# Branch B's K and Q turned by VectorE blocks and a trip through DRAM instead of by TensorE, in a two-layer mixer block

## The chip, the cores and the metric

The kernel runs on one core of one Trainium2 chip, as a single launch. The metric is the time of that launch on the device in microseconds (us). TensorE is PE in the rows, VectorE DVE, ScalarE ACT, GpSimd POOL and SyncE SP; PEld is the load of the stationary operand of a matmul.

## The reference, cut to what matters

Two layers act on 512 tokens of width 1024: 256 context tokens and 256 tokens of x. Each layer norms its input, multiplies it by one wide matrix w_in, and feeds three branches: A is a gated linear recurrence (mLSTM), B a differential attention, C a two-dimensional Fourier mix. The branches are merged through sigmoid gates and multiplied by w_out. The last layer returns x alone, so there only the x tokens have queries. Branch B, which the change touches:

```python
qh = apply_axial_rope(rmsnorm(q.reshape(b, n, 8, 2, 64), q_norm_w))   # 8 heads, 2 maps of 64 features
kh = apply_axial_rope(rmsnorm(k.reshape(b, n, 8, 2, 64), k_norm_w))
s = einsum('bhmqd,bhmkd->bhmqk', q, k) * 64 ** -0.5
p = softmax(s)
w = p[:, :, 0] - lam * p[:, :, 1]
o = einsum('bhqk,bhkv->bhqv', w, v)
y_b = rmsnorm(o, subln_w) * (1 - lam_init) * silu(bz)
...
y = g_a * (y_a @ w_a_out) + g_b * (y_b @ w_b_out) + g_c * (y_c @ w_c_out)
```

## The kernel before, in words

**Numbers.** Every fp32 operand of a large product is split into a high and a low float32r part, and a product is three matmuls (high by high, low by high, high by low). A split is a cast on ScalarE and a subtraction on VectorE (`split`).

**Main stream.** The weights come in pieces of 512 rows by 256 columns: a DMA of SP into `raw`, the cast `wh` on ScalarE, the subtraction `wl` on VectorE. A piece is multiplied with the 512 tokens (the last 256 in parts of layer 1) into one of three PSUM banks, whose tiles are called `pm`. The main stream goes through the branches in the order of ORDER0 and ORDER1; in layer 1 that is "A0 B0 A1 B1 A2 A3 C0 B2 B3 M0 C1 C2 C3 M1 M2 W0". A digit is a group of 256 columns; M0, M1 and M2 are the three merges (of branches A, B and C), W0 the last product.

**Side work.** What is no main product (branch B's scores and softmax, branch A's recurrence, branch C's transforms) is written as Python generators, which are launched when their projections are done. They use five other PSUM banks, whose tiles are called `ps`. While the program is written out, `Clocks` books each instruction on its engine at an estimated cost; after each main step `tick` lets a generator take its next step when the time it asked for (`when`) has been reached by the estimated TensorE clock. The order so found is fixed: every engine executes its own queue in that order, and waits on semaphores where the estimate was off. Every other engine's instruction is recorded by one helper (L161), every matmul at L232, every transpose on TensorE at L236.

**Branch B's side generator** is `b_side(g)`, for a group g of two heads. K and Q lie token-major, in [128 tokens, tiles, 256 features]. After norm and rope, `qk_transpose` turns them for one head: four transposes on TensorE (two for Q in layer 1) into a PSUM bank, and a split from the bank into `kT` and `qT`. For each query tile follow six matmuls of scores in two banks, the softmax (maximum on VectorE, exponential on ScalarE, the weighted difference `Pt` on VectorE), the transposes of `Pt` into `W` on TensorE, and the product `pv` of eight matmuls with V. A product pv comes up to LAG = 3 items behind its scores. At the end GpSimd makes the scale `os` of the outputs (tile `Q` in layer 1, where O lies in Q's place), VectorE applies it, TensorE transposes the outputs, and VectorE multiplies them into `Gb`, which is branch B's part of the merge.

**The merge** of branch i first runs its gates (products of `hTh`, `hTl` with weights) where AHEAD is 1, which it is for M1 of layer 1, then the products of the branch's output `y` with w_x_out. Between the two stands

```python
drain(recs)
```

which writes out all that is left of the branch's four side generators, one after the other, with no main step between.

**Memory.** `gen` hands out slots of one ring of SBUF tiles, NGEN = 28 of them, to all larger intermediates.

Of the kernel before, what the change touches and what calls it, by code (L numbers as in the profile page):

```python
# [27 lines left out]
NGEN = 28  # L28
# [4 lines left out]
ACTIVE = 5  # L33
# [8 lines left out]
ORDER1 = "A0 B0 A1 B1 A2 A3 C0 B2 B3 M0 C1 C2 C3 M1 M2 W0"  # L42
AHEAD = ((0, 1, 1), (1, 1, 0))
# [47 lines left out]
class Clocks:  # L91
    """When each engine gets to what is emitted, estimated, to place the side work among the main products."""
# [34 lines left out]
class Paced:  # L127
    """An engine whose instructions are booked as they are emitted."""
# [38 lines left out]
def hybrid_kernel(ctx: ExitStack, tc: tile.TileContext, t):  # L167
# [78 lines left out]
    # ------------------------------------------------------------- constants  # L246
# [117 lines left out]
    # ------------------------------------------------------------- adaLN  # L364
    def ada_bias(l, piece):
        """b_ada of 1024 columns in the first two rows of a tile of zeros"""
        brow = gen([128, 1024], F32, "brow")
        gpsimd.memset(brow, 0.0)
        gpsimd.dma_start(out=brow[0:2, :],
                            in_=t["b_ada"][l:l + 1, 512 * piece:512 * piece + 1024].to_broadcast([2, 1024]))  # L370
        return brow

    def ada_rows(l, piece, dma):
        """w_ada of 512 columns"""
        raws = []
        for q in range(4):
            r = gen([128, 2, 512], F32, "adaw")
            dma(out=r, in_=t["w_ada"][l, 256 * q:256 * (q + 1), 512 * piece:512 * (piece + 1)]
                .rearrange("(k p) f -> p k f", p=128))
            raws.append(r)  # L380
        return raws

    def ada_mm(raws, brow, dst):
        """sc @ w_ada + b_ada: partitions 32 g + stream hold four partial sums"""
        ps = ps_side()
        for k in range(KT):
            g = k % 4
            mm(ps[32 * g:32 * g + 32, :], sct[:, k, :], raws[k // 2][:, k % 2, :], k < 4, k >= 4)
        vector.tensor_tensor(dst, ps, brow, op=ALU.add)
# [8 lines left out]
    def ada_finish(l, pc, ks=slice(0, 8)):  # L398
        """pc: shift and scale of some blocks of features"""
# [9 lines left out]
    def ada_gen(l, pieces):  # L409
        """shift and scale columns (pieces 0..3) as a side generator"""  # L410
# [34 lines left out]
    # ------------------------------------------------------------- norm -> feature-major h  # L445
# [3 lines left out]
    def norm_stats(tiles):  # L449
        """normalized copies of some token tiles"""  # L450
# [10 lines left out]
    def norm_apply(l, i, src, base):  # L461
        """src: the normalized transposed blocks base .. base + 3 of token tile i; returns the closing step"""
# [23 lines left out]
    # ------------------------------------------------------------- weight pieces  # L486
# [74 lines left out]
    def fm_chunk(rhs, evac, ntok, bank=ps_main, step=4):  # L561
        """two 128-column blocks of W, feature-major: out[block][128 cols, tokens]"""
# [24 lines left out]
    def tm_chunk(lhs, tiles, evac, single=False, step=4):  # L587
        """256 columns of W, token-major: out[pair][128 tokens, 2, 256]"""
# [24 lines left out]
    # ------------------------------------------------------------- side machinery  # L613
# [4 lines left out]
    def launch(g):  # L618
        rec = {"g": g, "due": 0.0, "done": False}
        side.append(rec)  # L620
        return rec
# [8 lines left out]
    def tick():  # L630
        pe0 = clocks["pe"]
        for rec in list(side[:ACTIVE]):
# [12 lines left out]

    def hrhs(t0, n):
# [7 lines left out]
    # ============================================================= one layer  # L654
    def layer(l, P):
# [8 lines left out]
        def packed(name, i):  # L664
            """[128, 2, NTOK], two of them in a slot where they fit"""
# [6 lines left out]
        # ---------- branch A: gates  # L672
        def gates_side():
            """kind x head i of the gate preactivations: from column 32 x + i, token-major, to a partition"""
# [71 lines left out]
        # ---------- branch A: heads  # L746
# [72 lines left out]
        def a_side(h):  # L819
# [97 lines left out]
            for dh in range(2):  # L917
# [9 lines left out]
        # ---------- branch B  # L927
# [58 lines left out]
        def b_side(g):  # L986
# [25 lines left out]

            def qk_transpose(X, nt, n, name):
                ps = ps_side()
                for i in range(nt):
                    transpose(ps[:, 128 * i:128 * i + 128], X[:, i, 128 * hd:128 * hd + 128], ident)
                T = gen([128, 2, n], F32R, name)
# [6 lines left out]
            def softmax(hd, i, p2, n):  # L1024
                """the weighted difference of both maps, short of the first one's 1 / sum"""
# [8 lines left out]
                for m_ in range(2):  # L1034
# [9 lines left out]
                                               op0=ALU.mult, op1=ALU.add)  # L1044
                return Pt, ri, when(Pt)

            def w_transpose(Pt, n):
                ps = ps_side()
                for k in range(n // 128):
                    transpose(ps[:, 128 * k:128 * k + 128], Pt[:, 0, 128 * k:128 * k + 128], ident)  # L1050
                W = gen([128, 2, 512], F32R, "W")
# [18 lines left out]
            for it in items + [None] * LAG:  # L1070
                cur = None
                if it is not None and it[1] == 0:
                    hd = it[0]
                    kT = qk_transpose(K, 4, 512, "kT")
# [8 lines left out]
                if it is not None:  # L1083
# [13 lines left out]
                    pend.append((hd, i, Pt, at, n, ri[:, 0:1]))  # L1097
# [10 lines left out]
            for hd in range(2):  # L1108
# [8 lines left out]
        # ---------- branch C  # L1117
        def c_proj(g):
# [3 lines left out]
            def evu(a, pr, ps):  # L1122
                """sums and differences of features d and d + 128"""
# [64 lines left out]
        # ---------- merge  # L1188
        yacc = {}

        def merge(recs, ahead, key, first, final):
            ys = {}

            def split_y(q):
                ys[q] = gen_pair([128, 2, NTOK], "y")
                split(ST[key].pop(q), ys[q][0], ys[q][1])

            def spread(g, every):
                """split a y that is there after each so many steps"""
# [19 lines left out]
            drain(recs)  # L1219
# [65 lines left out]
    # ============================================================= program  # L1285
# [34 lines left out]
    # ---- start: the first products follow the adaLN columns, a quarter of the features at a time  # L1320
# [33 lines left out]
    def turn(q, hold=False):  # L1354
        """x, feature-major"""
# [13 lines left out]
    def quarter(q):  # L1369
        """the scale and shift of a quarter of the features, and what they make of x"""  # L1370
# [47 lines left out]
    def do(L, l, kind, i):  # L1418
# [10 lines left out]
        elif kind == "M":  # L1429
            recs = [ST[("a", "b", "c")[i], g]["rec"] for g in range(4)]  # L1430
            mo = [j for k, j in order[l] if k == "M"]
            run(L["merge"](recs, AHEAD[l][i], ("ya", "yb", "yc")[i], mo.index(i) == 0, mo.index(i) == 2))
# [63 lines left out]
```

## Time and profile before

| | |
|---|---|
| time, median of 3 runs | 1522.76 us (1522.59 to 1523.91) |
| span of the profiled execution | 1521.1 us, 25867 instructions |
| busy in it: TensorE | 1499.1 us, 99% |
| VectorE | 971.5 us, 64% |
| ScalarE | 735.0 us, 48% |
| GpSimd | 145.7 us, 10% |
| DMA, mean | 126 GB/s |

The span goes from the first to the last instruction of the profiled execution. No time of its own is given for that execution; the median of the runs is 1.7 us above its span. Busy times of TensorE overlap from one matmul to the next (each starts before the one ahead has ended), so the time that a matmul takes of the engine is read from the distance of starts.

### The profile page before, as it was taken

What the parts mean: (1) busy time and instruction counts of PE and PEld (TensorE: products, weight loads), DVE (VectorE), ACT (ScalarE), POOL (GpSimd) and SP (SyncE); (2) the same over time, 40 slices, a digit from 0 to 9 for tenths busy, and PEclk for the clock granted to TensorE, in tenths of its full rate; (3) what the DMA queues carried; (4) which work ended last, traced back from release to release, by engine and by line L of the source; (5) the groups of instructions that cost most, each with busy time, mean ns of one, the idle gap of its engine ahead of it and who ended that gap; (6) DMA issues with size and microseconds to landing.
All of it is one profiled execution on the core that took longest, in us unless ns stands there. A gap on an engine that the chain in (4) does not pass through costs nothing.

```text
span 1521.1 us, 25867 instructions
## 1 busy us (share of the span) xinstructions
PE 1499.1 (99%) x10410; PEld 1350.8 (89%) x10410; DVE 971.5 (64%) x1833; ACT 735.0 (48%) x1384; POOL 145.7 (10%) x193
## 2 busy tenths in 40 slices
PE   6999999999999999999999999999999999999999
PEld 4888889999998987897786789999999999999998
DVE  3447666677677586436664367677687666977765
ACT  4443556544544545334432235545557554656443
POOL 4001000020100010001024001001020011000200
PEclk9999999999999999999999999999999999999999
DMA  9524333332222222223249337544344523545754
GB/s 310 167 84 127 87 94 105 105 97 70 75 67 69 70 84 70 84 84 97 70 144 337 78 112 228 139 131 133 115 111 118 167 84 109 169 139 153 256 162 151
DMA packets 181611, 192.07 MB, mean 126 GB/s; under 512 B 9818, under 2 KB 174612, under 8 KB 181492
## 3 DMA queue, kind: packets, MB, share of 16 engines
q1 hardware_dynamic: 170080, 159.93, 35.6%
q0 software_dynamic: 7936, 27.27, 5.9%
q10 hardware_dynamic: 3476, 3.23, 0.7%
q8 instruction: 81, 1.33, 0.4%
q14 instruction: 38, 0.31, 0.1%
HBM read 188.23 MB, written 2.17 MB: 125 GB/s over the span
## 4 chain that ended last, share of the span: by engine, by line
PE 92%; DVE 3%; SPq 2%; issue 1%; ACT 1%; DMA 1%; ACTq 0%; DVEq 0%
PE pm L232 76%; PE ps L232 13%; PE ps L236 3%; SPq L161 2%; DVE wl L161 1%; DVE Rx L161 1%; DMA raw<-in_w_in_dram 0%; DVE Rc L161 0%; DMA prow<-in_a_norm_w_dram 0%; DVE lfm L161 0%; DVE at L161 0%; ACT lse L161 0%; DVE Ga L161 0%; ACT wh L161 0%; DVE ntmp L161 0%
## 5 line engine op out<-in xcount | busy, mean ns | idle before, releaser
L161 DVE TENSOR_TENSOR wl<-raw,wh 128x1024 fp32r<-128x1024 f32 x280 | 340.9, 1223 | 193.4 <-ACT wh L161 192.8
L161 ACT CAST wh<-raw 128x1024 fp32r<-128x1024 f32 x280 | 293.6, 1054 | 169.0 <-PE pm L232 135.0
L232 PE MATMUL pm<-hTh,wh 128*128 128x256 f32 (+1 forms) x1008 | 349.0, 346 | 0.0
L232 PE MATMUL pm<-hTl,wh 128*128 128x256 f32 (+1 forms) x1008 | 342.8, 340 | 0.0
L232 PE MATMUL pm<-hTh,wl 128*128 128x256 f32 (+1 forms) x1008 | 342.4, 340 | 0.0
L232 PE MATMUL pm<-wh,hTh 128*128 128x256 f32 (+1 forms) x1152 | 329.8, 286 | 1.5 <-DVE Ga L161 0.8
L232 PE MATMUL pm<-wl,hTh 128*128 128x256 f32 (+1 forms) x1152 | 324.1, 281 | 0.7 <-DVE wl L161 0.7
L232 PE MATMUL pm<-wh,hTl 128*128 128x256 f32 (+1 forms) x1152 | 324.2, 281 | 0.3 <-DVE hTl L161 0.2
L232 PEld LDWEIGHTS pm<-wh,hTh 128*128 128x128 f32 x1152 | 217.3, 189 | 10.4 <-issue 5.5
L232 PEld LDWEIGHTS pm<-wl,hTh 128*128 128x128 f32 x1152 | 216.9, 188 | 2.1 <-DVE wl L161 1.0
L232 PEld LDWEIGHTS pm<-wh,hTl 128*128 128x128 f32 x1152 | 217.5, 189 | 0.7 <-DVE hTl L161 0.7
L232 PEld LDWEIGHTS pm<-hTh,wh 128*128 128x128 f32 x1008 | 189.7, 188 | 30.8 <-issue 9.9
L232 PEld LDWEIGHTS pm<-hTh,wl 128*128 128x128 f32 x1008 | 189.5, 188 | 23.3
L232 PEld LDWEIGHTS pm<-hTl,wh 128*128 128x128 f32 x1008 | 189.7, 188 | 19.0
L232 PE MATMUL pm<-y,wh 128*128 128x512 f32 (+1 forms) x768 | 192.7, 342 | 0.0
L232 PEld LDWEIGHTS pm<-y,wh 128*128 128x128 f32 x768 | 128.9, 188 | 18.3 <-issue 2.6
L232 PE MATMUL pm<-y,wl 128*128 128x512 f32 (+1 forms) x384 | 129.4, 337 | 0.0
L161 ACT ACTIVATE Pt<-ps,mx,qsc 128x512 f32<-128x512 f32 (+1 forms) x96 | 67.1, 706 | 27.7 <-DVE mx L161 22.0
L232 PEld LDWEIGHTS pm<-y,wl 128*128 128x128 f32 x384 | 72.2, 188 | 8.6
L232 PE MATMUL pm<-wh,yf 128*128 128x256 f32 x384 | 73.0, 287 | 0.0
L232 PEld LDWEIGHTS pm<-wh,yf 128*128 128x128 f32 x384 | 59.9, 188 | 0.3
L161 DVE TENSOR_REDUCE mx<-ps 128x1 f32<-128x512 f32 (+1 forms) x96 | 53.0, 593 | 4.3 <-PE ps L232 4.2
(243 smaller groups left out, 1969.8 us busy)
## 6 DMA issues: line engine op xcount, KB each, us to landing
raw<-in_w_in_dram SPq DMA_DIRECT2D x192, 512.0 KB, 3.7
adaw<-in_w_ada_dram POOLq DMA_DIRECT2D x32, 512.0 KB, 7.1
raw<-in_w_out_dram SPq DMA_DIRECT2D x24, 512.0 KB, 4.5
adaw<-in_w_ada_dram SPq DMA_DIRECT2D x16, 512.0 KB, 8.5
raw<-in_w_in_dram SPq DMA_DIRECT2D x32, 256.0 KB, 3.3
raw<-in_w_a_out_dram SPq DMA_DIRECT2D x16, 512.0 KB, 3.4
raw<-in_w_c_out_dram SPq DMA_DIRECT2D x32, 256.0 KB, 3.4
raw<-in_w_b_out_dram SPq DMA_DIRECT2D x16, 512.0 KB, 3.8
```

What stands on the lines that cost most here:

```text
L161: return f(*a, **k)
L232: nc.tensor.matmul(out=o, lhsT=a, rhs=b, start=start, stop=stop)
L236: nc.tensor.transpose(o, a, idn)
```

## The change

- FLIP_K is set; the other three switches are off, so their branches write nothing. NGEN is 30, and the memory for GpSimd's DMA descriptors is given as 8192 bytes.
- After rope, each head of the group gets a tile `qkf` of [128, 1024]. One VectorE instruction (STREAM_TRANSPOSE) turns K of the head in blocks of 32 by 32 into the tile, a second one Q. A DMA of GpSimd writes each to a DRAM tile `flip`, and a second DMA reads it back into `qkf` in runs of 512 bytes such that each feature has a partition of its own.
- The first head's reads are issued when its writes are estimated to have landed; the second head's after the scores of the first head's last but one query tile.
- `qk_transpose` splits from `qkf` instead of from a PSUM bank.
- `drain_all` drains the same generators in the same order as before.

In counts: 112 transposes on TensorE go (64 of K, 48 of Q), 32 instructions come on VectorE, and 64 DMAs on GpSimd's queue, where there were 100.

```diff
-NGEN = 28
+NGEN = 30
+FLIP_H, FLIP_O, FLIP_K, FLIP_W = False,False,True,False
+FLIPB = 12
...
+    def flip_out(src, b):
+        groups = src.shape[1]
+        b = b.rearrange("p (b g j) -> p b g j", b=4, j=32)
+        vector.transpose(out=b.rearrange("p b g j -> p g b j"), in_=src.rearrange("p g (i b) -> p g b i", b=4))
+        d = dp.tile([128, 128 * groups], F32, tag="flip", name=nm("flip"), bufs=FLIPB)
+        gpsimd.dma_start(out=d, in_=b.rearrange("p b g j -> p (b g j)"))
+        return d
+
+    def flip_in(d, r):
+        gpsimd.dma_start(out=r.rearrange("p (a n) -> p a n", a=4), in_=d.rearrange("(a i) (b n) -> (i b) a n", a=4, b=4))
...
+    def split_turned(r, T):
+        split(r.rearrange("p (a g j) -> p g a j", a=4, j=32), *(T[:, z].rearrange("p (g a j) -> p g a j", a=4, j=32)
+                                                              for z in range(2)))
...
+            def qk_load(hd):
+                (dk, dq), b = flips[hd]
+                flip_in(dk, b[:, 0:512])
+                flip_in(dq, b[:, 512:512 + NTOK])
+                return b
+
+            flips, loads = [], {}
+            if FLIP_K:
+                for hd in range(2):
+                    b = gen([128, 1024], F32, "qkf")
+                    c = slice(128 * hd, 128 * hd + 128)
+                    flips.append(((flip_out(K[:, :, c], b[:, 0:512]), flip_out(Q[:, :, c], b[:, 512:512 + NTOK])), b))
+                yield when(*flips[0][0])
+                loads[0] = qk_load(0)
+
             def qk_transpose(X, nt, n, name):
+                T = gen([128, 2, n], F32R, name)
+                if FLIP_K:
+                    o = 512 * (name == "qT")
+                    split_turned(loads[hd][:, o:o + n], T)
+                    return T
                 ps = ps_side()
                 for i in range(nt):
                     transpose(ps[:, 128 * i:128 * i + 128], X[:, i, 128 * hd:128 * hd + 128], ident)
-                T = gen([128, 2, n], F32R, name)
                 split(ps[:, 0:n], T[:, 0, :], T[:, 1, :])
                 return T
...
                     hd = it[0]
+                    if FLIP_K:
+                        yield when(loads[hd])
                     kT = qk_transpose(K, 4, 512, "kT")
...
+                    if FLIP_K and (hd, i) == (0, NTL - 2):
+                        loads[1] = qk_load(1)
...
-            drain(recs)
+            drain_all(states)
...
-    nc = bacc.Bacc("TRN2", target_bir_lowering=False, num_devices=1)
+    nc = bacc.Bacc("TRN2", target_bir_lowering=False, num_devices=1, dynamic_dma_scratch_size=8192)
```

Since the estimated clocks see other instructions, the order of the queues changes at many places. Two of them matter below.

The first is TensorE's queue in layer 1, where M1's gates end and its products begin. `pm` is the main stream; `Q` of a transpose is the output tile O of branch B, `Pt` the softmax, `y` the branch's output. Before:

```order
L232 MATMUL pm_15041<-hTl,wh_14977 128x256
L232 MATMUL pm_15041<-hTh,wl_14978 128x256
L232 MATMUL ps_15166<-dft_1950_12905,U_14574 128x258 x6
L236 MATMUL ps_15177<-first_74,Q_13001 128x128 x2
L236 MATMUL ps_15181<-first_74,Q_13001 128x128 x2
L232 MATMUL pm_15185<-y_14742,wh_15044 128x256 x2
L232 MATMUL pm_15185<-y_14742,wl_15045 128x256
```

Now (of each product pv, of each set of scores and of each repeated round only the first row is shown):

```order
L234 MATMUL pm_14806<-hTh,wl_14773 128x256
L234 MATMUL ps_14919<-vt_12602,W_14875 128x256
...
L238 MATMUL ps_14933<-first_74,Pt_14621 128x128 x4
L234 MATMUL ps_14940<-vt_12603,W_14932 128x256
...
L238 MATMUL ps_14977<-first_74,Q_12254 128x128 x2
L238 MATMUL ps_14981<-first_74,Q_12254 128x128 x2
L234 MATMUL ps_14999<-kT_14993,qT_14996 128x512
...
L238 MATMUL ps_15020<-first_74,Pt_14720 128x128 x4
L234 MATMUL ps_15027<-kT_14993,qT_14996 128x512
...
L238 MATMUL ps_15126<-first_74,Q_12856 128x128 x2
L238 MATMUL ps_15130<-first_74,Q_12856 128x128 x2
L234 MATMUL pm_15134<-y_14518,wh_14809 128x256 x2
```

Between the last gate and the first product there stood the four transposes of one output tile (and six matmuls of branch C). Now 100 matmuls of groups 2 and 3 of branch B stand there, with no main product among them: for group 2 three products pv, two sets of transposes of Pt and the four transposes of the output; for group 3 two sets of scores, four sets of transposes of Pt, four products pv and the four transposes of its output.

The second is GpSimd's queue in layer 1, at the norms (`bst`) and outputs (`os`) of groups 2 and 3. Before:

```order
L161 TENSOR_TENSOR bst_13432<-bst_13432,chalf_87 128x16
L161 TENSOR_SCALAR bst_13432<-bst_13432 128x8
L161 TENSOR_TENSOR bst_13432<-bst_13432,chalf_87 128x8
L161 TENSOR_SCALAR os_13314<-os_13314 128x4
L161 TENSOR_TENSOR os_13314<-os_13314,chalf_87 128x4
```

Now:

```order
L163 TENSOR_TENSOR bst_13635<-bst_13635,chalf_87 128x16
L163 DMA flip_13673<-qkf_13671 128x512
L163 DMA flip_13676<-qkf_13671 128x256
L163 DMA flip_13680<-qkf_13678 128x512
L163 DMA flip_13683<-qkf_13678 128x256
L163 DMA qkf_13671<-flip_13673 128x4x128
L163 DMA qkf_13671<-flip_13676 128x4x64
L163 TENSOR_SCALAR bst_13635<-bst_13635 128x8
L163 TENSOR_TENSOR bst_13635<-bst_13635,chalf_87 128x8
L163 DMA qkf_13678<-flip_13680 128x4x128
L163 DMA qkf_13678<-flip_13683 128x4x64
```

The writes and reads of group 2 now stand ahead of the second half of group 3's norm, and a read waits at the head of the queue until its write has landed.

## Rows read from the trace of the kernel before

**Rows 1.** The profile page: the span, busy time of TensorE and VectorE (us, share of the span, instructions), DMA packets with the bytes moved, and the chain of work that ended last, as shares of the span by engine.

```profile
span 1521.1 us, 25867 instructions
...
PE 1499.1 (99%) x10410; PEld 1350.8 (89%) x10410; DVE 971.5 (64%) x1833; ACT 735.0 (48%) x1384; POOL 145.7 (10%) x193
...
DMA packets 181611, 192.07 MB, mean 126 GB/s; under 512 B 9818, under 2 KB 174612, under 8 KB 181492
...
PE 92%; DVE 3%; SPq 2%; issue 1%; ACT 1%; DMA 1%; ACTq 0%; DVEq 0%
```

**Rows 2.** Busy time by stretch (the windows view), the 20 us in which M1's gates run in layer 1: stretch, length, then busy us and instructions of PE, PEld, DVE, ACT, POOL, the granted clock, the share of the DMA engines and GB/s.

```profile
1390.00:1410.00 20.00, 20.00 (x173) 20.00 (x172) 13.38 (x24) 12.32 (x32) 0.00 (x0) 1.00 0.52 159
```

**Rows 3.** The timeline of TensorE in layer 0, at the first transposes of K and Q: start in us, length in us, engine, line, operation, tile written and tiles read, shape, count. Lengths overlap.

```profile
356.13 0.28 PE L232 MATMUL pm<-wh,hTl 128*128 128x256 f32 x1
356.25 0.60 PE L236 MATMUL ps<-first,K 128*128 128x128 f32 x4
356.68 0.60 PE L236 MATMUL ps<-first,Q 128*128 128x128 f32 x4
...
357.24 0.28 PE L232 MATMUL pm<-wl,hTh 128*128 128x256 f32 x1
```

**Rows 4.** The timeline of TensorE in layer 1, where M1's gates end: the transposes of the last output of branch B and the first product of M1.

```profile
1418.65 0.60 PE L236 MATMUL ps<-first,Q 128*128 128x128 f32 x4
1419.01 0.48 PE L232 MATMUL pm<-y,wh 128*128 128x256 f32 x2
```

**Rows 5.** The timeline of all engines in layer 1, one item of branch B from its product pv to the next W (columns as in rows 3; in brackets the idle time before and what ended it).

```profile
1397.75 1.03 PE L232 MATMUL ps<-vt,W 128*128 128x256 f32 x8
1397.80 0.16 DVE L161 RECIPROCAL ri<-ll 128x2 f32<-128x2 f32 x1
...
1398.25 0.75 DVE L161 SCALAR_TENSOR_TENSOR Pt<-Pt,ri 128x512 f32<-128x512 f32 x1
...
1398.78 0.28 PE L232 MATMUL pm<-hTl,wh 128*128 128x256 f32 x1
...
1399.01 0.60 PE L236 MATMUL ps<-first,Pt 128*128 128x128 f32 x4
1399.22 0.35 DVE L161 SCALAR_TENSOR_TENSOR Q<-ps,ri,Q 128x128 f32<-128x128 f32 x1 [0.21 <-ACT Q L161]
...
1399.57 0.28 PE L232 MATMUL pm<-hTl,wh 128*128 128x256 f32 x1
...
1400.51 0.69 DVE L161 TENSOR_TENSOR W<-ps,W 128x512 fp32r<-128x512 f32 x1 [0.94 <-ACT W L161]
```

**Rows 6.** The same view, the end of a group of branch B: its last product pv, the scale `os` on GpSimd and the outputs multiplied by it on VectorE.

```profile
1411.06 1.02 PE L232 MATMUL ps<-vt,W 128*128 128x256 f32 x8
...
1413.68 1.01 POOL L161 TENSOR_TENSOR os<-os,chalf 128x4 f32<-128x4 f32 x1
...
1416.48 0.68 DVE L161 TENSOR_TENSOR Q<-Q,os 128x512 f32<-128x512 f32 x1
```

**Rows 7.** The same view, further up in layer 1: two exponentials of one item and the reading of their sums, one set of scores with the main products around it, the maxima of one item.

```profile
1370.98 0.77 ACT L161 ACTIVATE Pt<-ps,mx,qsc 128x512 f32<-128x512 f32 x1
...
1372.41 0.19 ACT L161 ACTIVATION_READ_ACCUMULATOR Pt<-ps,mx,qsc 128x1 f32 x1
...
1378.16 0.28 PE L232 MATMUL pm<-wh,hTl 128*128 128x256 f32 x1
...
1378.37 0.96 PE L232 MATMUL ps<-kT,qT 64*128 64x512 f32 x6
...
1379.49 0.28 PE L232 MATMUL pm<-wl,hTh 128*128 128x256 f32 x1
...
1385.00 1.28 DVE L161 TENSOR_REDUCE mx<-ps 128x1 f32<-128x512 f32 x2
...
1386.32 0.16 DVE L161 TENSOR_TENSOR mx<-mx,qsc 128x2 f32<-128x2 f32 x1
```

**Rows 8.** Groups of instructions by line and shape: count, busy us, mean ns of one, idle time before and what ended it.

```profile
L161 DVE TENSOR_TENSOR kT<-ps,kT 128x512 fp32r<-128x512 f32 x16 | 11.0, 687 | 7.4 <-ACT kT L161 7.4
...
L161 DVE TENSOR_TENSOR K<-K,rtmp 128x512 f32<-128x512 f32 x8 | 5.5, 689 | 0.2
```

**Rows 9.** The timeline of TensorE at the start of the kernel (columns as in rows 3): the same two forms of instruction twice.

```profile
16.22 1.33 PE L236 MATMUL ps<-first,junk 128*128 128x128 f32 x5 [1.65 <-DVE junk L161]
17.48 1.94 PE L232 MATMUL ps<-adaw,sct 128*32 128x256 f32 x16
19.35 1.37 PE L236 MATMUL ps<-first,junk 128*128 128x128 f32 x8
...
21.37 1.07 PE L236 MATMUL ps<-first,junk 128*128 128x128 f32 x8
...
25.27 1.93 PE L232 MATMUL ps<-adaw,sct 128*32 128x256 f32 x32
```

**Rows 10.** DMAs by the queue that issues them: issues, KB each, median us from the issue to the landing; and GpSimd's time for an issue, from the groups of instructions (columns as in rows 8).

```profile
adaw<-in_w_ada_dram POOLq DMA_DIRECT2D x32, 512.0 KB, 7.1
...
Rb<-dR POOLq DMA_DIRECT2D x16, 448.0 KB, 5.3
...
xmid<-xn POOLq DMA_DIRECT2D x8, 128.0 KB, 3.9
...
L161 POOL DMA_DIRECT2D Rb<-dR x24 | 13.5, 564 | 1.8 <-PE ps L232 1.6
```

More of the change, by code (lines that the diff above doesn't have):

```diff
@@ L244, in split, with flip, gated @@
             vector.scalar_tensor_tensor(lo, src, scale, f32(hi), op0=ALU.mult, op1=ALU.subtract)
+    def flip_out(src, b):
[7 more added lines that the diff above has]
+        gpsimd.dma_start(out=r.rearrange("p (a n) -> p a n", a=4), in_=d.rearrange("(a i) (b n) -> (i b) a n", a=4, b=4))
+    def flip(src, name):
+        r = gen([128, 128 * src.shape[1]], F32, name)
+        d = flip_out(src, r)
+        yield when(d)
+        flip_in(d, r)
+        yield when(r)
+        return r
+    def split_turned(r, T):
+        split(r.rearrange("p (a g j) -> p g a j", a=4, j=32), *(T[:, z].rearrange("p (g a j) -> p g a j", a=4, j=32)
+                                                              for z in range(2)))
+    def gated(T, G):
+        t4 = T.rearrange("p (a i h j) -> p h i a j", a=4, h=2, j=32)
+        for h in range(2):
+            g = G[:, h, :].rearrange("p (i a j) -> p i a j", a=4, j=32)
+            vector.tensor_tensor(g, t4[:, h], g, op=ALU.mult)
+            yield 0
     xt = {}
@@ L616, in hybrid_kernel, with launch @@
     backlog = [0.0]
-    def launch(g):
-        rec = {"g": g, "due": 0.0, "done": False}
-        side.append(rec)
+    def launch(g, tail=False):
+        rec = {"g": g, "due": 0.0, "done": False, "tail": tail}
+        side.insert(0 if tail else len(side), rec)
         return rec
@@ L631, in tick @@
         pe0 = clocks["pe"]
-        for rec in list(side[:ACTIVE]):
+        tails = [r for r in side if r["tail"]]
+        for rec in tails + [r for r in side if not r["tail"]][:ACTIVE]:
             while not rec["done"] and rec["due"] <= clocks["pe"] < pe0 + SIDE_NS and \
@@ L644, in drain, with drain_all @@
                 step(r)
+    def drain_all(states):
+        for s in states:
+            drain([s["rec"]])
+            drain([s["tail"]] if "tail" in s else [])
     def hrhs(t0, n):
@@ L670, in packed, with tail @@
             return ST["half", name][:, 2 * (i % 2):2 * (i % 2) + 2, :]
+        def tail(s, key, g, src):
+            T = yield from flip(src, key + "T")
+            yield from gated(T, s["G"])
+            ST[key][g] = s["G"]
         def gates_side():
@@ L916, in a_side @@
             yield when(H)
-            for dh in range(2):
+            if FLIP_H:
+                s["tail"] = launch(tail(s, "ya", h, H[:, i0:4, :].rearrange("p i (h f) -> p (i h) f", h=2)), True)
+                return
+            for dh in range(0 if FLIP_H else 2):
                 ps = ps_side()
@@ L1044, in softmax @@
                                                op0=ALU.mult, op1=ALU.add)
+                if FLIP_W:
+                    return (flip_out(Pt[:, 0, 0:n].rearrange("p (g f) -> p g f", f=128), Pt[:, 1, 0:n]), Pt), ri, 0
                 return Pt, ri, when(Pt)
             def w_transpose(Pt, n):
+                W = gen([128, 2, 512], F32R, "W")
+                if FLIP_W:
+                    split_turned(Pt[:, 0, 0:n], W[:, :, 0:n])
+                    return W
                 ps = ps_side()
@@ L1050, in w_transpose @@
                     transpose(ps[:, 128 * k:128 * k + 128], Pt[:, 0, 128 * k:128 * k + 128], ident)
-                W = gen([128, 2, 512], F32R, "W")
                 split(ps[:, 0:n], W[:, 0, 0:n], W[:, 1, 0:n])
@@ L1096, in b_side @@
                     Pt, ri, at = yield from softmax(hd, i, p2, n)
-                    pend.append((hd, i, Pt, at, n, ri[:, 0:1]))
+                    pend.append([hd, i, Pt, at, n, ri[:, 0:1]])
+                    if FLIP_K and (hd, i) == (0, NTL - 2):
+                        loads[1] = qk_load(1)
+                for p in pend[:-1] if it is not None else pend:
+                    if FLIP_W and not p[3]:
+                        d, Pt = p[2]
+                        yield when(d, banks=0)
+                        flip_in(d, Pt[:, 0, 0:p[4]])
+                        p[2], p[3] = Pt, when(Pt, banks=0)
                 if cur is not None:
@@ L1107, in b_side @@
             yield when(O)
-            for hd in range(2):
+            if FLIP_O:
+                s["tail"] = launch(tail(s, "yb", g, ov), True)
+                return
+            for hd in range(0 if FLIP_O else 2):
                 ps = ps_side()
@@ L1189, in layer, with merge @@
         yacc = {}
-        def merge(recs, ahead, key, first, final):
+        def merge(states, ahead, key, first, final):
             ys = {}
             def split_y(q):
-                ys[q] = gen_pair([128, 2, NTOK], "y")
-                split(ST[key].pop(q), ys[q][0], ys[q][1])
+                yh, yl = ys[q] = gen_pair([128, 2, NTOK], "y")
+                y = ST[key].pop(q)
+                if key == "ya" and FLIP_H:
+                    for u in range(2):
+                        b = 8 * l + 2 * q + u
+                        split(y[:, u, :], yh[:, u, :], yl[:, u, :], scale=awcol[:, b:b + 1])
+                elif key == "yb" and FLIP_O:
+                    split(y, yh, yl, scale=slcol[:, l:l + 1])
+                else:
+                    split(y, yh, yl)
             def spread(g, every):
@@ L1429, in do @@
         elif kind == "M":
-            recs = [ST[("a", "b", "c")[i], g]["rec"] for g in range(4)]
+            states = [ST[("a", "b", "c")[i], g] for g in range(4)]
             mo = [j for k, j in order[l] if k == "M"]
-            run(L["merge"](recs, AHEAD[l][i], ("ya", "yb", "yc")[i], mo.index(i) == 0, mo.index(i) == 2))
+            run(L["merge"](states, AHEAD[l][i], ("ya", "yb", "yc")[i], mo.index(i) == 0, mo.index(i) == 2))
         else:
```

## The prediction

> **What bounds the kernel now.** I read the page first, then stretches, then single places. The page shows TensorE busy for 1499.1 us of a span of 1521.1, and 92% of the chain that ended last lies on it [rows 1]. The stretches say the same: in 1390 to 1410 TensorE works 20.00 of 20.00 us, while VectorE works 13.38 and ScalarE 12.32 [rows 2]. So the time is TensorE's queue, first row to last, and a change counts in two ways: by what it takes out of that queue, and by what it makes the queue wait for. The queue is in order. A side matmul costs its own time only if its operands are there when the queue comes to it.
>
> The place to look at is the end of M1's gates in layer 1, since the drain there writes out what branch B still has to do. Before, the four transposes of the last output start at 1418.65 and the first product of M1 at 1419.01, with no wait [rows 4]: branch B is finished with nothing to spare, and nothing is drained that isn't ready.
>
> **What is removed.** 8 transposes lie between the start at 356.25 and the second main matmul behind them at 357.24. A main matmul takes 0.12 us of the queue (356.13 to 356.25), and one of them is in that stretch, so the 8 take 0.87 us, 0.109 each [rows 3]. 112 go: 112 x 0.109 = **12.2 us off TensorE**, on the path everywhere. The Trainium skill ("VectorE: DVE Perf Modes", The three transpose paths) speaks against the change: it advises TensorE for a 128x128 transpose into PSUM and says that VectorE turns 32x32 blocks only. It prices the TensorE transpose at 390 ns (bf16); by that figure an estimate of the saving would be 43.7 us. The row decides for 12.2, since transposes follow each other faster than one lasts.
>
> **What is added beside other work.** VectorE gets 32 block transposes of up to 128x512. None is in the trace. The nearest rows are passes over 128x512 at 0.69 us [rows 8]; a lower end is half of that, an upper end four times (2.8), for the scattered writes. I take 0.7: 22 us on an engine that is busy for 64% [rows 1]. The casts and subtractions remain, now from SBUF; I cost them as before. GpSimd gets 64 DMAs at 0.56 us to issue [rows 10], 36 us on an engine that is busy for 10% [rows 1]. They move 7.3 MB out and 7.3 MB in, beside 192 MB [rows 1]. All this lies beside TensorE, and its cover is the work that stands in TensorE's queue meanwhile.
>
> A round trip is the price of that cover: two transposes 1.4, the issue of two writes 1.1, landing, the issue of two reads 1.1, landing. A landing is 3.9 us for 128 KB and 5.3 for 448 KB [rows 10]; I take 4.4 for 256 KB. Sum 1.4 + 1.1 + 4.4 + 1.1 + 4.4 = 12.4 us. In the new order some 15 us of TensorE's rows (the worth of 130 main matmuls at 0.12) stand between a group's block transposes and its first scores, so I cost the trip itself at nothing. If landings took 7.1, as the 512 KB ones do [rows 10], it would be 17.8 us and each of 8 groups could be late by 1 to 3 us; below nothing it cannot be. GpSimd's reads stand ahead of norms and of `os` and can hold those up by a landing; that is in the same bound. Ring slots: two more for the two `qkf` tiles of a group, nothing. The smaller descriptor memory: nothing, at most a delay of issues, in the same bound.
>
> **What is moved, the term that decides.** The trip, and the waits that the planner books for it, push each group's scores back. In the new order groups 2 and 3 are not done when M1's gates end: 100 side matmuls stand in a row ahead of the first product, and the first product cannot pass them. They form one chain from engine to engine:
>
> 1. A first product pv, 1.03 [rows 5].
> 2. Two items. From a pv's end (1398.78) through the output on ScalarE and VectorE, the square, the cast and the subtraction of the next W to its end (1401.20) are 2.42, and the next pv 1.03 [rows 5]: 3.45 each, 6.9. Now 7.9.
> 3. The end of group 2. From its pv's end (1412.08) to the end of `os` on GpSimd (1414.69) 2.61, the multiplication 0.68 [rows 6], the transposes 0.60 [rows 4]: 3.9. Now 11.8.
> 4. VectorE's queue behind it: two gatings of 128x256, the softmax difference (1397.80 to 1399.00, 1.20) [rows 5], the subtraction of kT 0.69 [rows 8] and of qT (128x256). The three of 128x256 lie between 0.35 (128x128) [rows 5] and 0.69; I take 0.45. Sum 3.2, and the last half of the scores 0.5. Now 15.5.
> 5. Maxima 1.28 and 0.16, two exponentials 1.62 (1370.98 to 1372.60) [rows 7], difference 1.20. Now 19.8.
> 6. Subtraction of W 0.69, the second scores' maxima, exponentials and difference, 4.3. Now 24.8.
> 7. Output on VectorE to W's end (1399.22 to 1401.20) 1.98, and pv 1.03 [rows 5]. Now 27.8.
> 8. Two more items 6.9, and the end of group 3, 3.9: **38.6 us**.
>
> TensorE's own work in it: 7 pv of 0.91, 8 sets of transposes of 0.44 [rows 5], 2 sets of scores of 1.0 (1378.37 to 1379.49, less a main matmul) [rows 7], together 11.9 us. The difference, **26.7 us, is new idle time**. Other matmuls cannot fill it, for the queue is in order. If every hand-over goes a little better, 20 is the least I can make of it; with longer waits between engines, 32.
>
> **The clock in that stretch.** At the start of the kernel TensorE waits more than it works, and the same instructions take twice as long as later: 5 transposes 1.33 us at 16.22, 8 of them 1.07 at 21.37; 16 adaLN matmuls 1.94 at 17.48, 32 of them 1.93 at 25.27 [rows 9]. That is the lower level, 1.2 GHz, though the granted clock of windows reads 1.00. In the chain TensorE works 11.9 of 38.6 us, so I expect it to fall there too. Then what it does on the chain itself takes twice as long: the last three pv (0.9 each), part of the scores (0.5), the last transposes (0.4), 3.6 us; and the first products behind it run at half speed until the clock is back. At the start that was between 19.35 (8 transposes 1.37) and 21.37 [rows 9], 3 to 5 us after dense work began; half of 3 us is lost. Together **5 us**. The bounds are nothing (no fall) and 7.
>
> **Sum.** 1521.1 - 12.2 + 26.7 + 5.0 = 1540.6. The median of the runs is 1.7 above the span, so **1542 us**. A measurement of this kernel can tell 0.2%, 3 us, from no change: faster means under 1519.7, slower over 1525.8.
>
> **The rivals.**
>
> - *The clock stays up* in the drain. For it: no row shows a fall once it had risen, and the windows read 1.00 [rows 2]. Against: the chain leaves TensorE without work for 3 to 5 us at a time (points 3, 4 and 7). Time 1537.
> - *The round trip is late in every group*: reads that land at 7 us, or block transposes at 2.8. TensorE would wait in front of the scores of 8 groups, 1 us each or more, on top of the drain: about 1550. For it: no row shows reads in runs of 512 bytes, and GpSimd's queue is in order. Against: some 3 us of slack in the order.
> - *Faster: the drain runs without gaps*, because the engines are ahead and its chain is no longer than TensorE's work. Then only the transposes count: 1521.1 - 12.2 + 1.7 = 1510.6. Its place is the first product of M1, its price the 26.7, and it decides from a chain of 24.1 us downwards (11.9 + 12.2): above that, the change is slower. Against it: every row of the chain was measured beside other work, and even without VectorE's backlog of point 4 the chain is 35. The Trainium skill's 390 ns would also end here, at 1479.1 without a drain and at about 1511 with one and the fallen clock.
> - *No change*: the chain is near 24 us, saving and idle time cancel: 1522.8.
>
> **How the numbers follow.** Forecast 0.52; clock stays up 0.28; late trips 0.10; faster 0.06; no change 0.04. So slower 0.90, same 0.04, faster 0.06. The range takes the first three: its lower end is 20 us of idle time at full clock, 1521.1 - 12.2 + 20 + 1.7 = 1531; its upper end is the forecast with late trips of 10, 1552.
>
> **What would show it.** Right: the first product of M1 stands behind a stretch of 38 to 44 us in which TensorE works about a third, with waits ended by VectorE and ScalarE, at pv, at the scores and at the outputs' transposes; everywhere else TensorE is busy as before; no transposes of K and Q; TensorE's instructions 112 fewer. Wrong: a drain below 24 us, or waits in front of the scores in layer 0, which has no such drain, or main matmuls that wait for `wl`. The clock part is wrong if the pv in the last third of the stretch take 1.0 us as before.

## The result, and the profile after

The change runs in 1544.89 us (1544.48 to 1546.88, 4 runs) against 1522.67 before (1522.5 to 1523.91): ratio 1.0147, 95% interval 1.0133 to 1.0162. The profiled execution has a span of 1542.7 us, 21.6 more than before.

The page of the changed kernel, with the lines that answer to [rows 1]; PEclk is the granted clock in tenths, in 40 slices of the span:

```profile
span 1542.7 us, 25855 instructions
...
PE 1500.7 (97%) x10298; PEld 1346.9 (87%) x10298; DVE 999.3 (65%) x1865; ACT 736.5 (48%) x1384; POOL 187.5 (12%) x257
...
PEclk9999999999999999999999999999999999996899
...
PE 88%; DVE 6%; ACT 3%; issue 1%; DMA 1%; POOL 1%; DVEq 0%; ACTq 0%; POOLq 0%
```

TensorE is busy for 1500.7 us, as much as before, though it has 112 transposes less: some of its rows now last twice as long (below). Its share of the chain fell from 92% to 88%, and VectorE's rose from 3% to 6%. Slice 37 of the clock reads 6, slice 38 reads 8. The windows there (columns as in [rows 2]):

```profile
1395.00:1410.00 15.00, 6.63 (x30) 4.69 (x30) 6.36 (x15) 5.33 (x17) 1.22 (x2) 0.63 0.11 36
1410.00:1420.00 10.00, 6.59 (x26) 4.22 (x24) 5.61 (x14) 3.99 (x10) 0.00 (x0) 0.50 0.00 0
1420.00:1430.00 10.00, 6.66 (x25) 5.28 (x25) 2.68 (x7) 3.36 (x11) 0.00 (x0) 0.50 0.00 0
1430.00:1440.00 10.00, 6.37 (x30) 5.92 (x30) 4.72 (x8) 2.84 (x6) 4.39 (x7) 0.51 0.37 114
1440.00:1450.00 10.00, 10.00 (x88) 10.00 (x88) 7.08 (x17) 3.97 (x10) 4.17 (x6) 1.00 0.96 331
```

From 1395 to 1440 TensorE works 26 of 45 us. The granted clock is 0.63 in the mean of the first 15 us and 0.50 behind them: the lower level, 1.2 GHz. It falls early (0.92 in 1398 to 1399, 0.50 in 1399 to 1400), when the longest wait of TensorE in the drain was 1.52 us so far. From 1440 on it is 1.00 and TensorE has no gap. This is the drain ahead of M1's products. Its timeline, TensorE alone (columns as in [rows 3]; in brackets the idle time before and what ended it); before, in [rows 4], the first product stood 0.36 us behind the start of its transposes:

```profile
1393.67 1.03 PE L234 MATMUL ps<-vt,W 128*128 128x256 f32 x8
1394.54 0.62 PE L238 MATMUL ps<-first,Pt 128*128 128x128 f32 x4
1396.68 0.39 PE L234 MATMUL ps<-vt,W 128*128 128x256 f32 x1 [1.52 <-ACT W L163]
...
1400.18 2.48 PE L234 MATMUL ps<-vt,W 128*128 128x256 f32 x8 [1.30 <-ACT W L163]
1406.16 1.08 PE L238 MATMUL ps<-first,Q 128*128 128x128 f32 x4 [3.50 <-DVE Q L163]
...
1409.53 1.22 PE L234 MATMUL ps<-kT,qT 64*128 64x512 f32 x4 [1.57 <-DVE kT L163]
...
1421.29 2.48 PE L234 MATMUL ps<-vt,W 128*128 128x256 f32 x8 [2.83 <-ACT W L163]
...
1425.53 2.48 PE L234 MATMUL ps<-vt,W 128*128 128x256 f32 x8 [0.88 <-ACT W L163]
...
1429.76 2.48 PE L234 MATMUL ps<-vt,W 128*128 128x256 f32 x8 [0.88 <-ACT W L163]
1435.73 1.09 PE L238 MATMUL ps<-first,Q 128*128 128x128 f32 x4 [3.49 <-DVE Q L163]
1436.47 0.78 PE L234 MATMUL pm<-y,wh 128*128 128x256 f32 x2
```

The stretch lasts from 1393.67 to 1436.47, 42.8 us. Behind the first, each pv waits for its W, each transpose of an output for VectorE's scaled Q. The eight matmuls of a pv take 1.03 at 1393.67 and 2.48 from 1400.18 on. The first products of M1 run at half speed too: 15 matmuls from 1436.47 to 1439.81, 3.3 us, which at 0.12 each would be 1.8. What TensorE waited for over the whole run (us in total, times, longest):

```profile
PE ps L234 <- ACT W L163: 8.5, 6, 2.8
...
PE ps L238 <- DVE Q L163: 7.0, 2, 3.5
...
PE pm L234 <- DVE wl L163: 1.9, 3, 0.9
...
PE ps L234 <- DVE kT L163: 1.6, 1, 1.6
...
PE ps L234 <- DVE W L163: 1.1, 2, 0.8
```

All but the third are the drain's, and the kernel before has none of those four; of the third it has one, of 0.7 us.

### The profile page after: what moved, and what is told of

Same layout as the page of the kernel before. It is cut to its first block, busy times and chain, and to the rows that moved or that the text cites. A ratio compares the mean times of both kernels' runs of the same rounds, so it can differ in the third digit from the quotient of the medians.

```text
span 1542.7 us, 25855 instructions
## 1 busy us (share of the span) xinstructions
PE 1500.7 (97%) x10298; PEld 1346.9 (87%) x10298; DVE 999.3 (65%) x1865; ACT 736.5 (48%) x1384; POOL 187.5 (12%) x257
## 4 chain that ended last, share of the span: by engine, by line
PE 88%; DVE 6%; ACT 3%; issue 1%; DMA 1%; POOL 1%; DVEq 0%; ACTq 0%; POOLq 0%
PE pm L234 73%; PE ps L234 13%; PE ps L238 2%; DVE wl L163 1%; DVE Rx L163 1%; ACT wh L163 1%; ACT junk L163 0%; DVE Rc L163 0%; DVE mx L163 0%; DMA crow<-in_c_dram 0%; ACT Pt L163 0%; DVE W L163 0%; DVE Q L163 0%; DVE lfm L163 0%; ACT Rb L163 0%
## 5 line engine op out<-in xcount | busy, mean ns | idle before, releaser
L234 PEld LDWEIGHTS ps<-vt,W 128*128 128x128 f32 x320 | 46.4, 206 | 16.2 <-ACT W L163 10.9
```

Source lines behind the costliest of these rows:

```text
L234: nc.tensor.matmul(out=o, lhsT=a, rhs=b, start=start, stop=stop)
```

## The experiments

The time of each is the median of its runs, the ratio is to the kernel before, measured on the same chip beside it: 1522.74 us for the change in one layer and the allowance of 3000 ns, 1522.86 for the slots, the lateness, fill_drain and swap_merges, 1523.99 for the others. Where times from different groups are compared, the ratios are the safer measure.

### The change in one layer only

```diff
             flips, loads = [], {}
-            if FLIP_K:
+            FLIPL = not last          # layer0_only; "last" in layer1_only
+            if FLIPL:
```

and FLIPL for FLIP_K in the three other places of `b_side`.

> K and Q turned by VectorE and DRAM in layer 0 alone; in layer 1 by TensorE as before. No stretch of side work alone stands in TensorE's queue. Theory (the trips are free where TensorE has other work, all of the loss is the drain in layer 1): 64 transposes x 0.109 = 7.0 us less than before, 1515.7. Rival (every group's trip costs a microsecond or more): 1520 to 1524.

> K and Q turned by VectorE and DRAM in layer 1 alone. The same 100 matmuls of branch B stand ahead of M1's products as in the change. Theory: the change without layer 0's saving of 7.0 us, 1544.9 + 7.0 = 1552. Rival (layer 0's trips cost as well): under 1545.

Measured: layer 0 alone **1515.05** us (1514.94 to 1515.91; ratio 0.9948, 0.9934 to 0.9963), layer 1 alone **1551.96** (1551.81 to 1552.33; 1.0190, 1.0173 to 1.0207). Both are where the theory had them within 1 us. Busy time of layer 0 alone:

```profile
span 1513.3 us, 25842 instructions
...
PE 1491.1 (99%) x10346; PEld 1343.7 (89%) x10346; DVE 987.3 (65%) x1849; ACT 735.5 (49%) x1384; POOL 167.3 (11%) x225
```

TensorE's 8.0 us less than before hold the 7.0 of the 64 transposes. So the trips cost nothing that shows in layer 0, the transposes are worth 0.12 us each (7.7 by 64, where the rows gave 0.109), and the whole loss is in layer 1. The change itself shows the same saving: the first main product of layer 1 that waits for its `wl` starts at 961.98, and at 969.70 before. The two differences add up: 1515.05 - 1522.74 = -7.7 and 1551.96 - 1522.74 = +29.2, together +21.5, against +22.2 for both layers at once.

### Slots and descriptor memory alone

```diff
-NGEN = 28
+NGEN = 30
...
-    nc = bacc.Bacc("TRN2", target_bir_lowering=False, num_devices=1)
+    nc = bacc.Bacc("TRN2", target_bir_lowering=False, num_devices=1, dynamic_dma_scratch_size=8192)
```

> The kernel before with 30 slots in the ring and 8192 bytes for descriptors, and nothing else. Theory: 1522.7 within 1.5. Rival (slots or descriptor memory carry part of the change): more than 3 us away.

Measured: **1522.75** us (1521.35 to 1523.91; ratio 0.9995, 0.9986 to 1.0004). They carry nothing of the change.

### Lateness without any trip

```diff
             yield when(K, Q)
+            yield after(18000.0)
```

> The kernel before, with no VectorE transposes and no trips: the planner is only told to wait 18 us between rope and K's transposes in every group of branch B. That leaves 64 side matmuls in a row ahead of M1's products (the last scores, four products pv with their transposes, the output). Theory (what costs is that branch B is late at the merge, whatever made it late): a chain of about 19 us with 7.6 us of TensorE's work in it, 11.5 us of new idle time, and 3 to 5 for the clock: 1535 to 1540. Rival (the trips cost, not the lateness): 1522.7.

Measured: **1544.73** us (1543.77 to 1546.98; ratio 1.0139, 1.0124 to 1.0154), above the expected 1535 to 1540. TensorE in that kernel, columns as above:

```profile
1414.43 0.78 PE L232 MATMUL ps<-T,dft 128*128 128x130 f32 x6
...
1418.27 1.40 PE L232 MATMUL ps<-vt,W 128*128 128x128 f32 x7 [1.28 <-DVE W L161]
...
1423.73 2.48 PE L232 MATMUL ps<-vt,W 128*128 128x256 f32 x8 [3.19 <-ACT W L161]
...
1438.13 1.09 PE L236 MATMUL ps<-first,Q 128*128 128x128 f32 x4 [3.47 <-DVE Q L161]
1438.87 0.78 PE L232 MATMUL pm<-y,wh 128*128 128x256 f32 x2
```

No VectorE transpose and no trip is in this kernel, yet a stretch of the same kind stands there, shorter (64 matmuls for 100), from 1414.43 to 1438.87, with the same waits and the same 2.48 us for a pv. Branch B is about as late as in the change: the last cast of `kT` starts at 1400.3, in the change at 1405.3, in the kernel before at 1351.8. So lateness alone costs this, whatever made branch B late. The size was too low: the stretch lasts 24.4 us where I had 19 and a few more for the clock. With 7.6 of work in it that is 16.8 of idle time, and some 1.8 of slow products behind it (the clock's mean is 0.87 from 1440 to 1450). The spans differ by 20.8 us. Of the rest, 1.8 lies ahead of the drain: the main stream stands that much later in the middle of layer 1 already (a product of 1252.44 at 1254.21), and in layer 0 the scores of one group wait 0.4 and 0.2 us for `qT`, with no trip in the kernel.

### What the clock costs

Matmuls whose results nobody reads were put into the drain, first behind every side step, then only where TensorE's next row waits for long:

```diff
             while not r["done"]:
                 step(r)
+                if filling[0] and not r["done"]:        # fill_drain
+                    bank = ps_main()
+                    for _ in range(3):
+                        mm(bank, hTh[:, 0, 0:128], hTh[:, 0, :], True, True)
```

```diff
                     W = w_transpose(cur[2], cur[4])
+                    fill(5)                             # fill_behind, the same matmuls
...
+                    fill(8)
                     yield when(*p2, banks=0)
...
+            fill(12)
             yield rstd_of(os_, 128, [128, NTL * 2])
...
+            fill(10 if g == 2 else 0)
             ST["yb"][g] = s["G"]
```

> The change, with three added matmuls of 512 columns into a spare bank of the main stream after each side step of the drain ahead of M1's products; nobody reads what they write. They take 0.66 us at full clock and run while TensorE would wait. Theory of the clock (the fall to 1.2 GHz costs 5 us of the drain): the clock stays at 1.00, the stretch shrinks from 42.8 to about 39 us, and the time goes to 1540, up to 1 us more where an added matmul stands in the way of the chain. Rival (the clock costs nothing, all is the chain of waits): 1545 or, by the added work, up to 1549.

> The change, with added matmuls of 512 columns into a spare bank of the main stream in the drain ahead of M1's products, as in fill_drain, but only where TensorE's next row waits anyway: 5 behind each set of transposes of Pt, 8 behind each set of scores, 12 ahead and 10 behind the transposes of an output; none between a product pv and the transposes behind it, where they stood in the chain before. Nobody reads them. Theory of the clock (its fall costs 5 us): the granted clock stays at 1.00, the stretch is about 39 us instead of 42.8, and the time 1539 to 1541. Rival (the fall costs nothing): 1545.

Measured: fill_drain **1546.39** us (1545.59 to 1547.62; ratio 1.0150, 1.0133 to 1.0167), fill_behind **1540.31** (1539.06 to 1542.43; 1.0108, 1.0093 to 1.0124). The first has the time that its rival foresaw (1545 to 1549), but it tells nothing of the clock's price. Its granted clock is 1.00 over the whole run, but here is one of its items (TensorE's timeline):

```profile
1397.24 0.39 PE L234 MATMUL ps<-vt,W 128*128 128x256 f32 x1
1397.97 1.02 PE L234 MATMUL ps<-vt,W 128*128 128x128 f32 x7 [0.34 <-DVE W L163]
1398.83 1.59 PE L234 MATMUL pm<-hTh 128*128 128x512 f32 x6
1400.26 0.60 PE L238 MATMUL ps<-first,Pt 128*128 128x128 f32 x4
...
1401.53 0.39 PE L234 MATMUL ps<-vt,W 128*128 128x256 f32 x1
```

Six added matmuls stand between a pv and the transposes of the next Pt, which then start 1.43 us later (1398.83 to 1400.26), and the cast of W waits for them: the added work sits in the chain. An item takes 4.29 us from pv to pv (1397.24 to 1401.53), as much as at half speed without it (1425.53 to 1429.76 in the change, 4.23). The second puts nothing there:

```profile
1393.74 1.03 PE L234 MATMUL ps<-vt,W 128*128 128x256 f32 x8
...
1396.75 0.38 PE L234 MATMUL ps<-vt,W 128*128 128x256 f32 x1 [0.36 <-ACT W L163]
...
1400.25 0.38 PE L234 MATMUL ps<-vt,W 128*128 128x256 f32 x1
...
1419.97 0.38 PE L234 MATMUL ps<-vt,W 128*128 128x256 f32 x1 [1.46 <-ACT W L163]
...
1423.98 1.88 PE L234 MATMUL ps<-vt,W 128*128 128x256 f32 x8
...
1432.83 0.63 PE L238 MATMUL ps<-first,Q 128*128 128x128 f32 x4 [0.69 <-DVE Q L163]
1433.22 0.48 PE L234 MATMUL pm<-y,wh 128*128 128x256 f32 x2
```

With the 80 added rows left out, TensorE's rows stand in the order of the change, one for one. The stretch is 39.5 us (1393.74 to 1433.22), 3.3 less than in the change. An item takes 3.50 us (1396.75 to 1400.25) where it took 4.23 at half speed, a pv takes what it took before (but for one of 1.88), and the first pair of products behind the stretch takes 0.48 where it took 0.78. The granted clock is below 1.00 in a part of 1420 to 1426 only (mean 0.72 there), so a little of its price is still in this time. By the spans 4.8 us are gained (1542.7 to 1537.9), by the medians 4.6, by the ratios 5.9; 5 were expected. So the fall of the clock is worth about 5 us of the change, and the rest of the stretch is waiting.

### The order of the merges

```diff
-ORDER1 = "A0 B0 A1 B1 A2 A3 C0 B2 B3 M0 C1 C2 C3 M1 M2 W0"
+ORDER1 = "A0 B0 A1 B1 A2 A3 C0 B2 B3 M0 C1 C2 C3 M2 M1 W0"
-AHEAD = ((0, 1, 1), (1, 1, 0))
+AHEAD = ((0, 1, 1), (1, 1, 1))
```

in the change (swap_merges) and in the kernel before (swap_merges_before).

> The change with branch C's merge ahead of branch B's in layer 1 (ORDER1 ends M2 M1 W0) and the gates of both run ahead of the drain. Branch B has one merge more to finish; no stretch of side work alone is left. Theory (drain): near 1510.5, up to 3 us more if another wait takes its place. Rival (the trips): 1520 or more.

> The kernel before with the same order of merges as swap_merges, its control. Theory (with no drain in either, the trips save the 112 transposes, 12.2 us, less what layer 1's start loses, about 1.4): 1516.65 + 11 = 1527 to 1529. Rival (the order itself gained, and the trips save less): 1522 or below.

Measured: **1516.65** us with the change (1516.12 to 1517.63; ratio 0.9953, 0.9938 to 0.9968) and **1524.92** without (1523.4 to 1526.39; 1.0008, 0.9999 to 1.0018). With branch B given one merge more of time, the same change gains: 0.9953 over 1.0008 is 0.9945, about 8.4 us in place of a loss of 22. It was expected to be 11. The two traces tell where it is lost. The wait for `wl` at the start of layer 1 stands at 963.06 with the change and at 969.37 without, 6.3 us apart, and the spans (1514.8 and 1521.6) differ by 6.8: in these two executions nearly all of the gain is layer 0's, and layer 1's 48 transposes bring 0.5 us of the 5.2 that they take of the queue. Layer 1 has 3.1 us of waits there that its control has not: 1.7 for `wh` and `wl` (as in the change, below), 0.9 among 30 matmuls of branch C which now stand alone ahead of M2's products, against the expectation that no such stretch is left, and 0.6 for an output of branch B. The rest is not placed.

### The planner's allowance

```diff
-BACKLOG1 = 1500.0
+BACKLOG1 = 3000.0        # 2300.0 in backlog_2300
```

> The change with one number of the planner altered: in layer 1, side steps may be written out while VectorE or ScalarE is estimated to be up to 3000 ns behind TensorE (1500 before). Branch B then ends before M1's gates do, and nothing is drained. Theory (drain): 1522.7 - 12.2 = 1510.5, within 2 us, and the granted clock is 1.00 throughout. Rival (the trips themselves, GpSimd's queue or DMA traffic): stays near 1545, or at least above 1520.

> The kernel before with the same number altered, as a control. Theory: TensorE is the bound and nothing was drained, so no change, 1522.7 within 1.5. Rival (the number itself gains several us): 1515 or less, and then the run of the change with it proves less.

> The change with the planner's number at 2300 ns, the least of those tried that leaves no drain. At 3000 the kernel before lost 13 us by the number itself. Theory (drain): between 1510.5 and 1520, clock at 1.00 at M1. Rival: 1540 or more.

Measured: the change with 3000 **1519.72** us (1518.47 to 1520.33; ratio 0.9977, 0.9968 to 0.9986), the kernel before with 3000 **1535.74** (1534.94 to 1536.61; 1.0083, 1.0068 to 1.0098), the change with 2300 **1528.58** (1527.01 to 1531.82; 1.0036, 1.0022 to 1.0050). All three forecasts missed: at 3000 the change is 9 us above the 1510.5, at 2300 it is 9 us above the upper end of 1520, and the control did not stay put, so the number has a price of its own. At the start of layer 1 the kernel before with 3000 is idle for 4.5 of 20 us, where the kernel before is for 1.5, and loses some of its clock (the rest of its 13 us was not placed):

```profile
960.00:980.00 20.00, 15.53 (x109) 15.10 (x109) 13.12 (x22) 10.41 (x23) 0.42 (x1) 0.86 0.40 108
```

So the gain of 25 us that the number brings to the change cannot be read as the price of the drain. With 2300 a smaller stretch of branch B (36 matmuls) is left at the same place, though none was expected, and its windows show the same signs:

```profile
1400.00:1420.00 20.00, 15.88 (x121) 14.72 (x119) 11.72 (x27) 9.53 (x26) 0.00 (x0) 0.90 0.24 79
1420.00:1440.00 20.00, 17.02 (x133) 17.05 (x134) 11.57 (x18) 6.16 (x8) 8.55 (x12) 0.85 0.85 300
```

These three runs agree with the drain, and alone would not prove it.

### Heavier trips

```diff
-        vector.transpose(out=b.rearrange(...
+        for _ in range(2):
+            vector.transpose(out=b.rearrange(...
...
-        gpsimd.dma_start(out=r.rearrange(...
+        for _ in range(2):
+            gpsimd.dma_start(out=r.rearrange(...
```

on top of layer0_only.

> As layer0_only, with each block transpose on VectorE done twice and each read back from DRAM done twice (the same data to the same place). Theory (VectorE's work and the trips lie beside TensorE's): 1515 within 1.5. Rival (they are only just hidden): each of layer 0's four groups 1 us or more later, 1519 or more.

Measured: **1519.95** us (1518.82 to 1520.78; ratio 0.9973, 0.9962 to 0.9984), where layer0_only has 0.9948: 3.8 us more. The time is the rival's, but not its reason, that each group is late. The scores of one group of the four are late, at 420 to 440, where TensorE waits for VectorE:

```profile
420.00:440.00 20.00, 17.60 (x100) 14.33 (x99) 17.18 (x41) 8.86 (x20) 0.00 (x0) 1.00 0.27 79
```

```profile
PE pm L234 <- DVE fold L163: 1.5, 1, 1.5
PE ps L234 <- DVE qT L163: 0.8, 1, 0.8
```

VectorE works 17.18 of those 20 us, and both `fold` (branch C's sums and differences, which VectorE reads out of a bank of the main stream) and the `qT` of a set of scores come late; these two waits are 2.3 us, and the rest of the 3.8 was not placed. As far as the waits show, the cover is wide in three groups and thin in one: the trip of the change is hidden, but not by far. Whether the doubled work of VectorE or the doubled reads did it was not separated; the waits point at VectorE.

## Why the prediction was right

**The sum.** Its terms, and what the traces have in their place:

| term | predicted | measured |
|---|---|---|
| 112 transposes | -12.2 | not measured as such; layer 0's 64: -7.7 where 7.0 were expected |
| chain of the drain at full clock | 38.6 | 39.5 (fill_behind, a part of 6 us of it below full clock) |
| the same with the clock down | 42.2 | 42.8 (1393.67 to 1436.47) |
| half speed behind it | 1.5 | 1.5 |
| waits elsewhere | 0 | 1.7 |
| span | 1540.6 | 1542.7 |

With the measured terms: 42.8 - 11.9 + 1.5 + 1.7 - 12.2 = 21.9, where the spans differ by 21.6. The 11.9 (TensorE's work in the drain) and the 12.2 are still the prediction's, so the agreement is good to about 1 us and no better. The drain was the step on which all hung, and it came from the order of the queue and from durations of single rows of before; the place, the waits and their releasers are as forecast. One of its signs of being right did not come as told: TensorE is busy for 24.05 of the 42.8 us there and not for a third, since its rows last longer at half speed; only their worth at full clock, 11.9, is near a third.

**The trip.** Its parts were priced from neighbours. In the changed kernel (counts, ns min, median, max, first and last start; then KB each and median us to the landing):

```profile
L163 POOL DMA_DIRECT2D flip<-qkf x32: 539/542/630, 357.8 to 1340.9; - x32
L163 POOL DMA_DIRECT2D qkf<-flip x32: 749/766/815, 361.3 to 1346.7; - x32
L163 DVE STREAM_TRANSPOSE qkf<-K x16: 1044/1083/1120, 356.4 to 1339.1; 128x512 f32<-128x512 f32 x16
L163 DVE STREAM_TRANSPOSE qkf<-Q x16: 581/820/1081, 357.5 to 1340.0; 128x512 f32<-128x512 f32 x8, 128x256 f32<-128x256 f32 x8
```

```profile
flip<-qkf POOLq DMA_DIRECT2D x24, 256.0 KB, 2.4
qkf<-flip POOLq DMA_DIRECT2D x24, 256.0 KB, 4.9
```

A block transpose of 128x512 takes 1.08 us where I took 0.7, within the bounds of 0.35 to 2.8; a write lands in 2.4 and a read in 4.9 where I took 4.4 for each. The parts add up to 12.1 us, where the sum for the trip was 12.4. An estimate by the Trainium skill's price of a TensorE transpose ("VectorE: DVE Perf Modes", The three transpose paths: 390 ns) would have been 25 us for layer 0's 64; 7.7 were measured, so the trace's 0.109 was the better price.

**The clock.** It fell as forecast, and was worth about 5 us where I had 5.0. That the size came out is in part luck: I had it fall late, with the last three pv at half speed and 0.9 us each, and it fell 5 us into the stretch, so five of the seven pv ran slow, but a slow item was only 0.73 us longer (4.23 for 3.50). The forecast rested on the kernel's first 25 us, where the windows read 1.00 and the rows last twice as long. The windows mislead there: in the trace of the kernel before, the record of the clock begins at 19.96 us, with 1.00, between the last slow row of [rows 9] (19.35) and the first fast one (21.37); of the time ahead of it the trace holds no clock. In the drain the record falls to 0.50 and rises again.

**What was not in it.** 1.7 us in the middle of layer 1, where a main product waits for a weight piece's cast and subtraction; "main matmuls that wait for `wl`" was one of the prediction's signs of being wrong, and it came in small:

```profile
1185.94 0.39 PE L234 MATMUL pm<-wh,hTh 128*128 128x256 f32 x1 [0.54 <-ACT wh L163]
1187.20 0.39 PE L234 MATMUL pm<-wl,hTh 128*128 128x256 f32 x1 [0.87 <-DVE wl L163]
...
1236.85 0.39 PE L234 MATMUL pm<-wl,hTh 128*128 128x256 f32 x1 [0.32 <-DVE wl L163]
```

These waits are there in layer1_only, in swap_merges and in fill_drain too, and not in layer0_only. Such waits need no trip, though: the kernel before with the allowance of 3000, in another order, waits 1.28 us for `wh` at 1197.79 and 0.76 for `wl` at 1199.05. Why the piece is late was not tested. So "the trip costs nothing" held in layer 0; in layer 1, with the merges swapped, new waits take back most of what the transposes save.

**The rivals.** The clock did not stay up. No group's scores waited outside the drain, so the trips were not late in every group. The drain had gaps, so it was not faster, and its 42.8 us are far from the 24 of no change. With no drain of branch B the change is a gain of 0.5% (swap_merges), nearly all of it from layer 0.

## What to carry to other kernels

When side work runs beside a busy engine by a fixed order, a change can take work off that engine and still lose, if it makes the side work end later than a point that the main work cannot pass. Look in the new order for rows of side work alone, add up their chain hand-over by hand-over, and compare it with the engine's own work in them. Here the change is a gain where there is slack (layer 0 alone: 1515.05 us) and a loss where there was none.

## What the runs showed of the hardware

- TensorE's clock was at 1.2 GHz from 1399 to 1440 us, in a stretch in which TensorE worked 26 of 45 us, most of that at half speed already, and came back 3.3 us into the dense products behind it. When it fell, TensorE had waited 1.52 us at most at a time in that stretch. Added matmuls in every gap kept it at 1.00 (fill_drain); added only in the long ones they kept it there but for a part of 6 us (fill_behind).
- VectorE's block transpose of 128x512 fp32 took 1.08 us, of 128x256 0.58, against 0.69 for a plain pass over 128x512 [rows 8].
- A write of 256 KB in rows of 2 KB landed 2.4 us after its issue, the read of the same bytes in runs of 512 bytes 4.9.
